# The first q panel projected one channel block at a time, the layer's embeddings projected later, and GpSimd's tensor work moved to VectorE

## The chip, the core and the metric

The kernel runs on one core of a Trainium2 chip. Its engines work at the same time, each through its own list of instructions in order: TensorE (PE; its weight loads are shown as PEld), VectorE (DVE), ScalarE (ACT), GpSimd (POOL) and SyncE (SP), whose queue starts all of this kernel's transfers. The metric is the device time of one execution, in microseconds (us).

## The reference, cut to what matters

One decoder layer on 512 tokens of 1024 channels, in float32:

```python
h  = rmsnorm(x, g_mix);  z = h @ w_in            # 1024 -> 9728 columns
rq, rk, rv, rg, aq, ak, av, gl = split(z)
y  = rmsnorm(retention(rotate(rq), rotate(rk) * dk**-0.5, rv), ret_gn)    # 4 heads, chunks of 128
ret_branch = (silu(rg) * y) @ w_ret_out
aq, ak = rotate(rmsnorm(aq, q_gain)), rotate(rmsnorm(ak, k_gain))         # 3 groups of 4 heads of 128
att_branch = merge_by_denominators(dilated_window_attention(...) for 3 groups) @ w_att_out
x  = x + (sigmoid(g_r) * ret_branch + sigmoid(g_a) * att_branch) @ w_o
x  = x + square(relu(rmsnorm(x, g_mlp) @ w_up)) @ w_down
x  = x + sigmoid(rmsnorm(x, g_ple) @ w_ple_gate) * (p @ w_ple_proj)
```

`p` holds 256 embedding channels a token. `p @ w_ple_proj` depends on nothing else in the layer and is used only in the last line.

## The kernel before, in words

**Products.** Every product is made three times (`mm3`, L258 to L260): both operands are split into a rounded high part and the rest, and high x high, high x low and low x high are added up in one bank of PSUM. A weight arrives as a unit of 512 KB (`raw`, two or four blocks of 128 channels) and is split by `split_unit`: `whi` on ScalarE (L225), `wlo` on VectorE (L226). Six `raw` buffers and four pairs of `whi` and `wlo` are turned over, so a unit's transfer waits until an earlier unit has been split.

**Panels.** A panel is 512 output columns for all 512 tokens: 4 token tiles x 8 channel blocks x 3 = 96 products in `rows_gemm`, in two halves of four channel blocks; in the second half each token tile is finished in turn and given to `consume`. Four PSUM banks (`pg`) hold the four token tiles, and a bank is free for the next panel when `consume` has read it. The order of the panels is q, k, v for each of the three attention groups, then the retention's panels.

**The first normalization** is not applied to x before the projection. The panel is computed on x times the gain, and the token's factor `r` (`token_factors`: four squares on ScalarE with a running sum, L489, then a power on GpSimd, L493) scales each bank when it is read (`zn`, L558).

**After a q or k panel**, `consume` squares each head of `zn` (L562), takes the root on GpSimd (`rstd`, L357), scales (L564) and rotates: t1 = zn x C on GpSimd (L513), two half products with S on VectorE (L516), their sum on VectorE (L518). C and S are tables made on GpSimd (`tables`, L542) from rotation constants (`rotc`) and the gains (in `mg`). The heads are then transposed on TensorE (`heads_T`, L528).

**Delayed work.** `later(lag, ...)` puts a step into a queue; `tick`, called between groups of products, takes at most one ripe step out. The heads' transposes of a panel so fall into the second half of the next one, and a group's scores, probabilities (`pe`, `pT`) and values (`po`, L643) into the panels after its v panel.

**The start.** `setup` loads the embeddings' columns, both units of `w_ple_proj`, x by channels (four loads of 512 KB), two units of the q panel and x by tokens. `embed` splits the embeddings, then alternates the split of x (`hh` L469, `hl` L470) with the split of the q panel's units, and projects the embeddings in eight bank fills of six products, which are evacuated and stored to DRAM (`pp_dram`). Only then come `token_factors`, the tables and the q panel.

The instructions stand on each engine in the order that the tile framework's scheduler chose when the kernel was built, which need not be the order in which the code is written.

Of the kernel before, what the change touches and what calls it, by code (L numbers as in the profile page):

```python
# [24 lines left out]
H = 4  # L25
# [6 lines left out]
WARM = 4  # L32
# [43 lines left out]
class Block:  # L76


    def __init__(self, ctx, tc, a):
# [17 lines left out]
        self.pinned = False  # L97
        self.plan, self.raws, self.loaded, self.used = [], [], [], 0
# [118 lines left out]
    def split_unit(self, raw, g0):  # L217
# [5 lines left out]
        if g0 is None:  # L223
            for i in range(k) if self.pinned else [slice(0, k)]:
                self.pin(nc.scalar.activation(R(hi[:, i]), raw[:, i], AF.Copy))  # L225
                nc.vector.tensor_tensor(R(lo[:, i]), raw[:, i], hi[:, i], op=ALU.subtract)  # L226
# [35 lines left out]
    def rows_gemm(self, act, nk, consume, perm=False, group=2, need=None, wave=None, halves=False):  # L262
# [3 lines left out]
        if wave is not None:  # L266
            us = []

            def part(t, u):
                if u == 0:  # L270
                    banks[t] = self.gbank()
                wh, wl = us[u]
                for k in range(2):
                    kk = 2 * u + k
                    sh, sl = self.stat(act, kk, t, perm)
                    self.mm3(banks[t], sh, sl, wh[:, k], wl[:, k], kk == 0, kk == nk - 1)
                if u == nu - 1:
                    consume(t, banks[t])

            for m in range(NT):  # L280
                self.pinned = True
                if m >= 2:
                    wave(m)
                us += self.units(1)
                if m < NT - 1:
                    for t in range(m):
                        part(t, m)
                self.force(("h", m, 1))
                if m < NT - 1:
                    for u in range(m + 1):  # L290
                        part(m, u)
                self.pinned = False
            for t in range(NT - 1):
                part(t, NT - 1)
                part(NT - 1, t)
                self.ahead(t + 1)
            part(NT - 1, NT - 1)
            return
# [105 lines left out]
    def setup(self):  # L404
        nc, a = self.nc, self.a
        self.p_raw = self.wraw.tile([P, 1024], F32, tag="raw", name="p_raw").rearrange("p (k t) -> p k t", k=2)
        for k in range(2):
            nc.sync.dma_start(self.p_raw[:, k], a["p_cols"][k * P : (k + 1) * P])
        self.fetch(2)
# [3 lines left out]
        self.x_cols = []  # L413
# [42 lines left out]
    def embed(self):  # L456
        nc = self.nc
        pT = self.big("pT")
        hi, lo = pT[:, 0:2], pT[:, 2:4]
        self.pinned = True  # L460
        for k in range(2):
            self.pin(nc.scalar.activation(R(hi[:, k]), self.p_raw[:, k], AF.Copy))
            nc.vector.tensor_tensor(R(lo[:, k]), self.p_raw[:, k], hi[:, k], op=ALU.subtract)
        self.ahead(2)
        self.hT = self.new_act(2, "h")
        for k in range(KD):
# [4 lines left out]
            if k % 2:  # L471
                self.ahead(2 + (k + 1) // 2)
        self.pinned = False
        self.pp_dram = self.dram.tile([S, D], F32, name="pp_dram", tag="pp_dram")
# [32 lines left out]
    def rotate(self, zn, C, Sn):  # L507
# [5 lines left out]
        nc.gpsimd.tensor_tensor(v4(t1), v4(zn), bc(C, HD), op=ALU.mult)  # L513
# [24 lines left out]
    def tables(self, g, n):  # L538
        C = self.tabp.tile([P, NT, HD], F32, tag="tab", name=self.nm("C"))
        Sn = self.tabp.tile([P, NT, HD], F32, tag="tab", name=self.nm("S"))  # L540
        for o, part, gi in ((C, 0, 2 * n), (Sn, 1, 2 * n + 1)):
            ins = self.nc.gpsimd.tensor_tensor(  # L542
                o, self.rc[:, 0, :, part * HD : (part + 1) * HD],
                self.gains[:, gi, g * HD : (g + 1) * HD].unsqueeze(1).to_broadcast([P, NT, HD]), op=ALU.mult)
            if g == 0:
                self.tc.keep_in_program_order(ins)
        return C, Sn

    def att_proj(self, g, n, **kw):
        nc = self.nc  # L550
        tabs = [] if kw else [self.tables(g, n)]
# [19 lines left out]
        self.rows_gemm(self.hT, KD, consume, **kw)  # L571
# [32 lines left out]
    def attention(self, g, **kw):  # L604
        nc = self.nc
        qT = self.att_proj(g, 0, **kw)
# [58 lines left out]
    def merge(self, groups, oh, ol):  # L665
# [32 lines left out]
        def weigh(h, g):  # L698
# [11 lines left out]
            nc.gpsimd.tensor_tensor(n, accs[h], t, op=ALU.add)  # L710
# [24 lines left out]
    def retention(self):  # L735
# [10 lines left out]
        def decayed(t, k):  # L746
            if t < NT - 1:
                nc.gpsimd.tensor_tensor(v4(kd[:, t]), v4(k), kdec.unsqueeze(2).to_broadcast([P, H, HD]), op=ALU.mult)

        qT = self.ret_proj()  # L750
        for h in range(H):
            def cross(h=h):
                v = lambda t: t[:, h, P:].rearrange("p (n i) -> p n i", i=P)
                nc.gpsimd.tensor_tensor(v(qd), v(qT), qdec[:, h].unsqueeze(1).to_broadcast([P, NT - 1, P]), op=ALU.mult)
# [261 lines left out]
    def make_plan(self):  # L1016
        a, w = self.a, self.w_in
        for half in range(2):
            self.plan_rows(a["w_ple_proj"][0], 512 * half, 2)
        for g in range(NG):  # L1020
            for c in (AQ, AK, AV):
                self.plan_rows(w, c + 512 * g, KD)
        for c in (RQ, RK, RV, RG, RV + 512, RG + 512):
# [12 lines left out]
    def run(self):  # L1036
# [36 lines left out]
```

## Time and profile before

| | us |
|---|---|
| median of 3 runs (lowest, highest) | 1042.34 (1041.96, 1045.39) |
| the profiled execution, its own time | 1040.62 |
| its span, first to last instruction | 1038.9 |
| mean granted TensorE clock | 0.993 |
| TensorE busy | 1009.2 |
| VectorE busy | 664.1 |
| ScalarE busy | 460.5 |
| GpSimd busy | 142.0 |
| GpSimd: L513, L542, L710, L754, L748 (59 tensor operations) | 92.1 |

The page gives busy time by engine, the chain of work that ended last, and the costliest groups of instructions. A row of the timeline reads: start, duration, engine, line, operation, output<-inputs, shape, count, and in brackets how long the engine had been idle and what ended that. In a row of a stretch stand the busy time of TensorE, its weight loads, VectorE, ScalarE and GpSimd, each with the number of instructions, then the granted TensorE clock, the share of time that the transfer engines were busy, and GB/s. A row of waits gives the total, how often, and the longest.

### The profile page before, as it was taken

How to read it: one execution, taken by the hardware profiler on the slowest of the kernel's cores; microseconds unless marked ns; L12 is line 12 of the kernel's file. 1: busy time of each engine (PE TensorE's matmuls, PEld its weight loads, DVE VectorE, ACT ScalarE, POOL GpSimd, SP SyncE). 2: the span in 40 equal slices, each digit the busy share in tenths (PEclk: the TensorE clock that was granted, in tenths of full speed). 3: DMA queues.
4: the chain of work that ended last, by engine and by line, in shares of the span. 5: the costliest groups of instructions: out<-in, count | busy, mean ns of one | idle time of the engine just before them, and what ended most of it. 6: DMA issues, size and time to landing. Idle time of an engine off the chain costs nothing.

```text
span 1038.9 us, 12633 instructions
## 1 busy us (share of the span) xinstructions
PE 1009.2 (97%) x4772; PEld 847.0 (82%) x4772; DVE 664.1 (64%) x912; ACT 460.5 (44%) x901; POOL 142.0 (14%) x123
## 2 busy tenths in 40 slices
PE   5998989999999899999999999999999999999998
PEld 3787878988988788888888888988888888888877
DVE  5388675667586634546444444679768877967983
ACT  5443634364352332434232323565356355355461
POOL 0264043223025500000000000000000000000000
PEclk9999999999999999999999999999999999999999
DMA  9842312213321222222323422354753753845711
GB/s 345 226 136 66 100 41 77 87 61 103 101 63 59 81 82 81 82 81 62 101 82 109 175 81 82 102 183 157 231 177 117 250 163 122 261 164 180 247 63 58
DMA packets 85756, 130.90 MB, mean 126 GB/s; under 512 B 7360, under 2 KB 39616, under 8 KB 85696
## 3 DMA queue, kind: packets, MB, share of 16 engines
q1 hardware_dynamic: 85696, 130.10, 38.9%
q8 instruction: 37, 0.61, 0.3%
q14 instruction: 23, 0.19, 0.1%
HBM read 125.87 MB, written 4.21 MB: 125 GB/s over the span
## 4 chain that ended last, share of the span: by engine, by line
PE 85%; DVE 7%; issue 2%; DMA 2%; POOL 2%; ACT 1%; SPq 0%; ACTq 0%; DVEq 0%; POOLq 0%
PE pg L258 25%; PE pg L260 25%; PE pg L259 25%; DVE wlo L226 2%; PE pb L260 2%; PE pb L259 2%; PE pb L258 2%; DVE ro L516 1%; PE ph L528 1%; DMA raw<-in_w_in 1%; PE pt L367 1%; POOL r L357 1%; DMA xr<-in_x_cols 1%; PE po L643 1%; PE sc L620 1%
## 5 line engine op out<-in xcount | busy, mean ns | idle before, releaser
L226 DVE TENSOR_TENSOR wlo<-raw,whi 128x1024 fp32r<-128x1024 f32 (+1 forms) x200 | 246.2, 1244 | 97.5 <-ACT whi L225 95.9
L225 ACT ACTIVATE whi<-raw 128x1024 fp32r<-128x1024 f32 (+1 forms) x200 | 203.7, 1031 | 232.9 <-PE pg L260 101.3
L258 PE MATMUL pg<-whi,hh 128*128 128x512 f32 x480 | 201.5, 420 | 0.1
L259 PE MATMUL pg<-wlo,hh 128*128 128x512 f32 x480 | 189.2, 394 | 1.1 <-DVE wlo L226 1.1
L260 PE MATMUL pg<-whi,hl 128*128 128x512 f32 x480 | 189.0, 394 | 0.0
L357 POOL TENSOR_TENSOR r<-v,mhalf 128x4 f32<-128x4 f32 (+1 forms) x48 | 38.3, 798 | 609.7 <-DVE v L356 609.5
L260 PEld LDWEIGHTS pg<-whi,hl 128*128 128x128 f32 x480 | 98.7, 206 | 17.5
L259 PEld LDWEIGHTS pg<-wlo,hh 128*128 128x128 f32 x480 | 99.2, 207 | 15.1 <-DVE wlo L226 1.6
L258 PEld LDWEIGHTS pg<-whi,hh 128*128 128x128 f32 x480 | 98.9, 206 | 14.0 <-ACT zn L558 0.5
L258 PE MATMUL pg<-h2h,whi 128*128 128x512 f32 (+1 forms) x288 | 105.4, 367 | 0.0
L259 PE MATMUL pg<-h2l,whi 128*128 128x512 f32 (+1 forms) x288 | 105.2, 365 | 0.0
L260 PE MATMUL pg<-h2h,wlo 128*128 128x512 f32 (+1 forms) x288 | 105.2, 365 | 0.0
L259 PEld LDWEIGHTS pg<-h2l,whi 128*128 128x128 f32 x288 | 54.3, 189 | 8.8
L258 PEld LDWEIGHTS pg<-h2h,whi 128*128 128x128 f32 x288 | 54.2, 189 | 8.8
L260 PEld LDWEIGHTS pg<-h2h,wlo 128*128 128x128 f32 x288 | 54.3, 189 | 8.6
L258 PE MATMUL pg<-hh,whi 128*128 128x512 f32 x128 | 52.5, 410 | 0.0
L260 PE MATMUL pg<-hh,wlo 128*128 128x512 f32 x128 | 50.0, 390 | 0.0
L259 PE MATMUL pg<-hl,whi 128*128 128x512 f32 x128 | 49.9, 390 | 0.0
L258 PE MATMUL pg<-whi,uh 128*128 128x512 f32 x128 | 49.9, 390 | 0.0
L260 PE MATMUL pg<-whi,ul 128*128 128x512 f32 x128 | 49.9, 390 | 0.0
L259 PE MATMUL pg<-wlo,uh 128*128 128x512 f32 x128 | 49.8, 389 | 0.0
L207 DVE TENSOR_TENSOR raw<-raw,raw 128x1024 f32<-128x1024 f32 x32 | 39.0, 1220 | 12.2 <-DMA raw<-in_w_down 12.2
(179 smaller groups left out, 1761.6 us busy)
## 6 DMA issues: line engine op xcount, KB each, us to landing
raw<-in_w_down SPq DMA_DIRECT2D x80, 512.0 KB, 3.4
raw<-in_w_in SPq DMA_DIRECT2D x76, 512.0 KB, 3.8
raw<-in_w_up SPq DMA_DIRECT2D x32, 512.0 KB, 5.1
x<-in_x SPq DMA_DIRECT2D x8, 512.0 KB, 8.6
raw<-in_w_ret_out SPq DMA_DIRECT2D x8, 512.0 KB, 3.4
raw<-in_w_o SPq DMA_DIRECT2D x8, 512.0 KB, 3.4
raw<-in_w_ple_gate SPq DMA_DIRECT2D x8, 512.0 KB, 4.5
xr<-in_x_cols SPq DMA_DIRECT2D x4, 512.0 KB, 8.0
```

The source lines that it names most:

```text
L207: self.nc.vector.tensor_tensor(raw, raw, g0, op=ALU.add)
L225: self.pin(nc.scalar.activation(R(hi[:, i]), raw[:, i], AF.Copy))
L226: nc.vector.tensor_tensor(R(lo[:, i]), raw[:, i], hi[:, i], op=ALU.subtract)
L258: t.matmul(ps, sh, mh, start=first, stop=False, skip_group_check=more)
L259: t.matmul(ps, sh, ml, start=False, stop=False, skip_group_check=more)
L260: t.matmul(ps, sl, mh, start=False, stop=last, skip_group_check=more)
L357: self.nc.gpsimd.tensor_tensor(r, v, self.mhalf[:, :w], op=ALU.pow)
L367: nc.tensor.transpose(ps[:, k * P : (k + 1) * P], part[:, k * P : (k + 1) * P], self.ident)
L516: nc.vector.tensor_tensor(v4(t2)[:, :, o0 : o0 + 64], v4(zn)[:, :, i0 : i0 + 64], bc(Sn[:, o0 : o0 + 64], 64), op=ALU.mult)
L528: self.nc.tensor.transpose(ps[:, t * P : (t + 1) * P], rots[t][:, h * HD : (h + 1) * HD], self.ident)
L620: nc.tensor.matmul(sc[:, h * P : (h + 1) * P], qT[:, h, rs], kT[:, h, rs], start=True, stop=True)
L643: nc.tensor.matmul(po[:, h * P : (h + 1) * P], v[:, vt, h * HD : (h + 1) * HD], pt, start=b == 0, stop=b == len(blocks) - 1)
```

## The change

Four things are changed.

1. The q panel of the first group is made by a new function, `first_panel`. The loads of x and of the panel's four units are cut into blocks of 128 channels (256 KB each) and issued in turn, x block, weight block. Through a `hook` in `split_unit` each x block is split just ahead of its weight block. The panel's products go through the first four channel blocks with all four token tiles before the second four are taken tile by tile. `token_factors` is called between these halves.
2. `embed` is called after the first group's v panel. Its loads of p and `w_ple_proj` stand in the plan behind that panel, and its pieces are split whole. The branch of `rows_gemm` for `wave`, which nothing called, is removed.
3. The tensor operations of GpSimd, except the powers and one add, go to VectorE: t1 of the rotations (32), the tables (12), the merge's adds (8), the decayed k (3) and q (4). The add that makes `gm` in `mix` stays on GpSimd.
4. Ten warm products instead of four.

```diff
@@ setup
-        self.p_raw = self.wraw.tile([P, 1024], F32, tag="raw", name="p_raw").rearrange("p (k t) -> p k t", k=2)
-        for k in range(2):
-            nc.sync.dma_start(self.p_raw[:, k], a["p_cols"][k * P : (k + 1) * P])
-        self.fetch(2)
...
         for u in range(KD // 2):
-            v = xr[u // 2][:, 2 * (u % 2) : 2 * (u % 2) + 2]
-            nc.sync.dma_start(v, a["x_cols"][256 * u : 256 * (u + 1)].rearrange("(k p) t -> p k t", p=P))
-            self.x_cols += [v[:, 0], v[:, 1]]
-        self.fetch(4)
+            src, _ = self.plan[u]
+            raw = self.wraw.tile([P, 1024], F32, tag="raw", name=self.nm("raw")).rearrange("p (k n) -> p k n", k=2)
+            for k in range(2):
+                c = slice((2 * u + k) * P, (2 * u + k + 1) * P)
+                nc.sync.dma_start(self.x_cols[2 * u + k], a["x_cols"][c])
+                nc.sync.dma_start(raw[:, k], src[k * P : (k + 1) * P])
+            self.raws.append((raw, None))
@@ split_unit
             for i in range(k) if self.pinned else [slice(0, k)]:
+                if self.hook is not None:
+                    self.hook(i)
@@ first_panel (new)
+        self.pinned = True
+        for u in range(KD // 2):
+            self.hook = lambda i: split_x(2 * u + i)
+            us += self.units(1)
+        self.hook = None
+        self.pinned = False
+        banks = [self.gbank() for _ in range(NT)]
+        for k in range(KD // 2):
+            for t in range(NT):
+                part(t, k)
+        self.token_factors()
+        for t in range(NT):
+            for k in range(KD // 2, KD):
+                part(t, k)
+            consume(t, banks[t])
+            self.ahead(1 + t // 2)
+            self.tick()
@@ embed
+        raw = self.big("praw")[:, 0:2]
+        nc.sync.dma_start(raw, self.a["p_cols"].rearrange("(k p) t -> p k t", p=P))
         hi, lo = pT[:, 0:2], pT[:, 2:4]
+        nc.scalar.activation(R(hi), raw, AF.Copy)
+        nc.vector.tensor_tensor(R(lo), raw, hi, op=ALU.subtract)
@@ rotate (and in the same way: tables, weigh, decayed, cross)
-        nc.gpsimd.tensor_tensor(v4(t1), v4(zn), bc(C, HD), op=ALU.mult)
+        nc.vector.tensor_tensor(v4(t1), v4(zn), bc(C, HD), op=ALU.mult)
@@ run
-        self.embed()
-        self.token_factors()
         self.load_tables()
-        groups = [self.attention(g) for g in range(NG)]
+        groups = []
+        for g in range(NG):
+            groups.append(self.attention(g))
+            if g == 0:
+                self.embed()
```

How the instructions stand on the engines, at three places. In the rows, `whi` and `raw` are a weight unit and its load, `hh` the split x, `j` with `ss` a square of an x tile (with x) or of a head (with zn), numbers tell buffers apart.

ScalarE between the end of the splits and the first `zn`, before:

```order
L225 ACTIVATE whi_170<-raw_168 128x512 x2
L469 ACTIVATE hh_141<-xr_94,gcol 128x512 x2
L489 ACTIVATE j_270,ss_269<-x_103 128x1024 x2
L143 ACTIVATE pp_216<-pg_209 128x512
L143 ACTIVATE pp_236<-pg_229 128x512
L489 ACTIVATE j_270,ss_269<-x_104 128x1024 x2
L143 ACTIVATE pp_256<-pg_249 128x512
L225 ACTIVATE whi_182<-raw_180 128x512 x2
```

and with the change:

```order
L433 ACTIVATE hh_146<-xr_87,gcol 128x512
L228 ACTIVATE whi_179<-raw_103 128x512
L484 ACTIVATE j_242,ss_241<-x_108 128x1024
L228 ACTIVATE whi_293<-raw_291 128x1024
L484 ACTIVATE j_242,ss_241<-x_108 128x1024
L484 ACTIVATE j_242,ss_241<-x_109 128x1024 x2
L228 ACTIVATE whi_363<-raw_361 128x1024
L552 ACTIVATE zn_269<-pg_189,r 128x512
```

The evacuations of the embedding are gone from between the squares, and between the first and the second square now stands the split of the k panel's first unit, `raw_291`.

SyncE's queue from the x tiles to the k panel's units, before:

```order
L423 DMA x_104<-in_x 128x1024 x2
L191 DMA raw_168<-in_w_in 128x2x512
L191 DMA raw_180<-in_w_in 128x2x512
L191 DMA raw_350<-in_w_in 128x2x512
L191 DMA raw_356<-in_w_in 128x2x512
L191 DMA raw_495<-in_w_in 128x2x512
L479 DMA pp_dram<-pp_196 128x512
L191 DMA raw_501<-in_w_in 128x2x512
L440 DMA rotc_283<-in_c_rot 128x4x256 x2
```

and with the change:

```order
L392 DMA x_109<-in_x 128x1024 x2
L409 DMA rotc_134<-in_c_rot 128x4x256 x2
L413 DMA mg_137<-in_c_mask 128x512
L417 DMA mg_137<-in_q_gain 128x384
L419 DMA mg_137<-in_q_gain 128x3x64 x2
L417 DMA mg_137<-in_k_gain 128x384
L419 DMA mg_137<-in_k_gain 128x3x64 x2
L192 DMA raw_291<-in_w_in 128x2x512
L192 DMA raw_361<-in_w_in 128x2x512
```

The first k units (`raw_350` and `raw_356` before) stood ahead of the tables, the mask and the gains; now (`raw_291`, `raw_361`) they stand behind all of them.

VectorE's rotation of the first token tile of the first q panel, before:

```order
L356 TENSOR_SCALAR v_382<-ss_374 128x4
L564 TENSOR_TENSOR zn_376<-zn_376,r_383 128x512
L516 TENSOR_TENSOR ro_388<-zn_376,S_295 128x4x64 x2
L518 TENSOR_TENSOR ro_389<-ro_387,ro_388 128x512
L356 TENSOR_SCALAR v_414<-ss_406 128x4
```

and with the change:

```order
L326 TENSOR_SCALAR v_275<-ss_267 128x4
L558 TENSOR_TENSOR zn_269<-zn_269,r_276 128x512
L508 TENSOR_TENSOR ro_284<-zn_269,C_280 128x512
L511 TENSOR_TENSOR ro_285<-zn_269,S_281 128x4x64 x2
L513 TENSOR_TENSOR ro_286<-ro_284,ro_285 128x512
L326 TENSOR_SCALAR v_317<-ss_309 128x4
```

One operation is added to each tile's chain on VectorE, t1 (L508), which GpSimd did beside the two half products.

More of the change, by code (lines that the diff above doesn't have):

```diff
@@ L31 @@
 NEG = -3.0e38
-WARM = 4
+WARM = 10
 GG = (2, 4)
@@ L260, in mm3, with rows_gemm @@
         t.matmul(ps, sl, mh, start=False, stop=last, skip_group_check=more)
-    def rows_gemm(self, act, nk, consume, perm=False, group=2, need=None, wave=None, halves=False):
+    def rows_gemm(self, act, nk, consume, perm=False, group=2, need=None, halves=False):
         banks = [None] * NT
         nu = nk // 2
[L266 to L272, printed above, removed]
-                for k in range(2):
[L274 to L298, printed above, removed]
         for u0 in range(0, nu, group):
@@ L453, in load_tables, with first_panel, split_x @@
         self.gains = gv
-    def embed(self):
+    def first_panel(self, consume):
         nc = self.nc
[L458 to L464, printed above, removed]
         self.hT = self.new_act(2, "h")
-        for k in range(KD):
+        us = []
+        def split_x(k):
             g = self.gcol[:, k : k + 1]
@@ L470, in embed, with part @@
             nc.vector.scalar_tensor_tensor(R(l), self.x_cols[k], g, h, op0=ALU.mult, op1=ALU.subtract)
-            if k % 2:
-                self.ahead(2 + (k + 1) // 2)
-        self.pinned = False
+        self.pinned = True
+        for u in range(KD // 2):
+            self.hook = lambda i: split_x(2 * u + i)
+            us += self.units(1)
+        self.hook = None
+        self.pinned = False
+        banks = [self.gbank() for _ in range(NT)]
+        def part(t, k):
+            wh, wl = us[k // 2]
+            sh, sl = self.stat(self.hT, k, t, False)
+            self.mm3(banks[t], sh, sl, wh[:, k % 2], wl[:, k % 2], k == 0, k == KD - 1)
+        for k in range(KD // 2):
[8 more added lines that the diff above has]
+            self.tick()
+    def embed(self):
+        nc = self.nc
+        pT = self.big("pT")
+        raw = self.big("praw")[:, 0:2]
+        nc.sync.dma_start(raw, self.a["p_cols"].rearrange("(k p) t -> p k t", p=P))
+        hi, lo = pT[:, 0:2], pT[:, 2:4]
+        nc.scalar.activation(R(hi), raw, AF.Copy)
+        nc.vector.tensor_tensor(R(lo), raw, hi, op=ALU.subtract)
         self.pp_dram = self.dram.tile([S, D], F32, name="pp_dram", tag="pp_dram")
@@ L541, in tables, with att_proj @@
         for o, part, gi in ((C, 0, 2 * n), (Sn, 1, 2 * n + 1)):
-            ins = self.nc.gpsimd.tensor_tensor(
+            self.nc.vector.tensor_tensor(
                 o, self.rc[:, 0, :, part * HD : (part + 1) * HD],
                 self.gains[:, gi, g * HD : (g + 1) * HD].unsqueeze(1).to_broadcast([P, NT, HD]), op=ALU.mult)
-            if g == 0:
-                self.tc.keep_in_program_order(ins)
         return C, Sn
-    def att_proj(self, g, n, **kw):
+    def att_proj(self, g, n):
         nc = self.nc
-        tabs = [] if kw else [self.tables(g, n)]
+        lazy = g == 0 and n == 0
+        tabs = [] if lazy else [self.tables(g, n)]
         rots = []
@@ L602, in transpose4, with attention @@
         return pT
-    def attention(self, g, **kw):
+    def attention(self, g):
         nc = self.nc
-        qT = self.att_proj(g, 0, **kw)
+        qT = self.att_proj(g, 0)
         kT = self.att_proj(g, 1)
@@ L709, in weigh @@
             n = self.tmp("mt")
-            nc.gpsimd.tensor_tensor(n, accs[h], t, op=ALU.add)
+            nc.vector.tensor_tensor(n, accs[h], t, op=ALU.add)
             accs[h] = n
@@ L1017, in make_plan @@
         a, w = self.a, self.w_in
-        for half in range(2):
-            self.plan_rows(a["w_ple_proj"][0], 512 * half, 2)
         for g in range(NG):
@@ L1022, in make_plan @@
                 self.plan_rows(w, c + 512 * g, KD)
+            if g == 0:
+                for half in range(2):
+                    self.plan_rows(a["w_ple_proj"][0], 512 * half, 2)
         for c in (RQ, RK, RV, RG, RV + 512, RG + 512):
```

13 lines of the change are left out of this document (8 added, 5 removed).

## The prediction

> **What bounds the kernel now.** I read the page's busy line and chain first, then TensorE's own waits, then the timeline of the first 110 us.
>
> ```profile
> span 1038.9 us, 12633 instructions
> PE 1009.2 (97%) x4772; PEld 847.0 (82%) x4772; DVE 664.1 (64%) x912; ACT 460.5 (44%) x901; POOL 142.0 (14%) x123
> PE 85%; DVE 7%; issue 2%; DMA 2%; POOL 2%; ACT 1%; SPq 0%; ACTq 0%; DVEq 0%; POOLq 0%
> PE pg L258 <- ACT pp L143: 4.5, 1, 4.5
> PE po L643 <- DVE pT L147: 4.4, 1, 4.4
> PE pg L258 <- ACT whi L225: 4.3, 1, 4.3
> PE ph L528 <- DVE mt L705: 3.8, 2, 3.3
> PE pg L258 <- DVE pp L147: 3.7, 1, 3.7
> ```
>
> TensorE is the bound, 85% of the chain. No product is removed, so only its idle time and its slow-clock time can be won: three waits in the embedding projection (12.5 us), one on the first attention group's probabilities (4.4), one at the merge (3.8).
>
> ```profile
> 32.72 0.39 PE L258 MATMUL pg<-whi,hh 128*128 128x512 f32 x1
> 54.48 0.39 PE L258 MATMUL pg<-whi,hh 128*128 128x512 f32 x1
> 105.47 0.40 PE L258 MATMUL pg<-whi,hh 128*128 128x512 f32 x1
> ```
>
> These rows are the first products of the first q panel, of the first k panel, and of the second group's q panel. A panel's 96 products take 21.76 us, 0.227 each. The embedding's 48 would take 10.9, yet q starts at 32.72: some 21 us of TensorE are lost before it. I measure the change by when the second group's q panel would start, now 105.47.
>
> **The change part by part.** *First panel by channel blocks.* Per block of 128 channels ScalarE does one hh and one whi, VectorE one hl and one wlo:
>
> ```profile
> 16.31 1.32 ACT L469 ACTIVATE hh<-xr,gcol 128x512 fp32r<-128x512 f32 x2
> 17.54 1.13 ACT L225 ACTIVATE whi<-raw 128x512 fp32r<-128x512 f32 x2
> 17.13 1.41 DVE L470 SCALAR_TENSOR_TENSOR hl<-xr,gcol,hh 128x512 fp32r<-128x512 f32 x2
> 18.46 1.28 DVE L226 TENSOR_TENSOR wlo<-raw,whi 128x512 fp32r<-128x512 f32 x2
> 0.00:10.00 10.00, 4.25 (x10) 2.28 (x11) 4.12 (x7) 4.95 (x8) 0.74 (x7) 1.00 0.79 266
> 10.00:20.00 10.00, 5.90 (x20) 4.36 (x18) 5.83 (x10) 5.98 (x11) 0.00 (x0) 0.99 1.04 400
> 20.00:24.00 4.00, 2.93 (x6) 1.82 (x6) 1.24 (x3) 1.21 (x3) 0.00 (x0) 0.59 1.04 388
> ```
>
> Halved: 1.23 us of ScalarE and 1.35 of VectorE a block; 0.52 MB at 388 GB/s (last column) is 1.35 too. TensorE needs 12 x 0.227 = 2.7 a block in the first half, so it is fed. First block complete near 7 us, panel end 7 + 21.8 = 28.8, where it was 54.48. Taken alone, and with the embedding's 10.9 added back later, that would be 14.8 us won. A slow clock at the start could cost some us here, but the next wait covers it. The six added warm products lie ahead of any data: nothing.
>
> *What is late next: the token factors r.* They move behind the first half of the panel, and no bank of q can be evacuated without them (zn, scaled by r). The order rows above show ScalarE's program: one square, then whi of the k panel's first unit, then three squares. That unit's load stands on SP's queue behind the x tiles, the rotation tables, the mask and six gain loads. So r waits for a weight unit, and the unit for the gains. Bytes ahead of the gains: 4.2 (panel and x) + 2.1 + 1.05 + 0.26 = 7.65 MB; 2.66 + 4.00 MB are moved by 20 us, the rest takes 2.5: 22.5. Then the gains, 0.79 MB in 256- and 1536-byte pieces. The nearest rows are the same loads in the kernel before:
>
> ```profile
> 37.50:43.50 6.00, 6.00 (x28) 4.99 (x27) 0.00 (x0) 1.06 (x1) 0.00 (x0) 1.00 0.79 68
> 44.50:50.50 6.00, 6.00 (x28) 4.98 (x27) 3.11 (x4) 3.56 (x15) 3.72 (x3) 1.00 0.39 102
> 46.03 1.00 SPq L191 DMA_DIRECT2D raw<-in_w_in  x2
> 50.50:56.00 5.50, 5.50 (x26) 4.57 (x25) 4.22 (x8) 3.43 (x10) 2.89 (x3) 1.00 0.96 355
> raw<-in_w_in SPq DMA_DIRECT2D x76, 512.0 KB, 3.8
> ```
>
> Weight units issued at 46.03 were not moved before about 50.5: while the gains ran the queue gave 102 GB/s, afterwards 355. At 388 GB/s the gains would cost 2.0 us (lower end), at 102 they cost 7.7 (taken: same loads, same queue), at 68, a stretch that also holds the r store, 11.6 (upper end). The unit itself moves in 1.35, and I add 1.2 for its end (a lone unit lands 3.8 after issue, 2.4 of it not moving; half, an estimate). It lands at 22.5 + 7.7 + 1.35 + 1.2 = 32.8 (27.1 to 36.7).
>
> ```profile
> 28.62 1.06 ACT L489 ACTIVATE j<-x 128x1024 f32<-128x1024 f32 x1
> 29.80 1.06 ACT L489 ACTIVATE j<-x 128x1024 f32<-128x1024 f32 x1
> 31.31 1.03 POOL L493 TENSOR_TENSOR r<-v,mhalf 128x4 f32<-128x4 f32 x1 [30.01 <-DVE v L492]
> ```
>
> From there whi 1.0, three squares at 1.18 (28.62 to 29.80), v and the power 1.6: 6.2 us. Call the time of r **A**: 39.0 (33.3 to 42.9). TensorE, done at 28.8, stands idle to A + 0.7 and starts the k panel at a low clock; both lie under what follows.
>
> *VectorE's rotations.* They now start at A, not during the panel, and the heads' transposes in the k panel wait for the fourth.
>
> ```profile
> 60.30 0.16 DVE L356 TENSOR_SCALAR v<-ss 128x4 f32<-128x4 f32 x1
> 61.58 0.69 DVE L564 TENSOR_TENSOR zn<-zn,r 128x512 f32<-128x512 f32 x1 [1.12 <-POOL r L357]
> 62.31 1.86 DVE L516 TENSOR_TENSOR ro<-zn,S 128x256 f32<-128x256 f32 x2
> 64.27 0.69 DVE L518 TENSOR_TENSOR ro<-ro,ro 128x512 f32<-128x512 f32 x1
> 64.88 0.16 DVE L356 TENSOR_SCALAR v<-ss 128x4 f32<-128x4 f32 x1
> 298.97 1.28 POOL L513 TENSOR_TENSOR ro<-rz,rotc 128x512 f32<-128x512 f32 x1 [2.04 <-issue]
> 300.38 0.75 DVE L516 TENSOR_TENSOR ro<-rz,rotc 128x256 f32<-128x256 f32 x2
> ```
>
> A tile took 64.88 - 60.30 = 4.58. GpSimd's t1 goes to VectorE (0.61, as L518's spacing), but the L516 pair takes 0.75 where GpSimd has just ended (300.25) and 1.86 beside it: 4.58 + 0.61 - 1.11 = 4.08 a tile. So GpSimd's work costs VectorE nothing in these chains. From A: zn and its squares 2.1, four tiles 16.3, two wlo 2.3, a table 0.6: fourth rotation at A + 21.3. Then four heads (0.44) each with six products (1.37): k panel ends A + 28.5. VectorE's next four tiles end near A + 44.5, where TensorE's v panel (16.3 in) needs them: no wait. v ends at A + 28.5 + 23.5 = A + 52.0.
>
> *Embedding behind v.* Its raw load queues on SP behind two weight loads that wait for buffers which the second wlo of w_ple_proj frees, near A + 47; with their 2.7 us of moving and its own it lands near A + 51.5, and split by A + 53.7: 2 us of wait (0 to 4). Then 10.9 for the products; scores and evacuations run beside it. Second group's q: A + 64.9 = 103.9, where it was 105.47: **-1.6**.
>
> *Later stalls.*
>
> ```profile
> 152.08 1.29 PE L643 MATMUL po<-pT,v 128*128 128x128 f32 x8 [4.38 <-DVE pT L147]
> 155.00:160.00 5.00, 5.00 (x21) 4.09 (x20) 0.00 (x0) 1.04 (x1) 0.00 (x0) 0.86 0.00 0
> 343.27 0.66 PE L528 MATMUL ph<-ident,ro 128*128 128x128 f32 x4 [3.33 <-DVE mt L705]
> 345.00:350.00 5.00, 5.00 (x20) 4.04 (x20) 2.67 (x4) 2.36 (x4) 4.92 (x4) 0.75 0.67 191
> L710 POOL TENSOR_TENSOR mt<-mt,mt 128x512 f32<-128x512 f32 x8 | 13.3, 1658 | 14.1 <-DVE mt L705 13.9
> ```
>
> At 152 the pT copy stood behind the last of four rotations. The group's steps now begin in the embedding, so it stands behind the first: TensorE waits about 1.4 instead of 4.4, and keeps its clock (the row at 0.86 lost 0.7 in 5 us; I take twice that from 152 on): **-4.4**. At the merge the eight adds (1.66 each on GpSimd) become 0.61 on VectorE without the trips between, while VectorE takes 11 us more work there and loses some 6 of contention: I take half of 3.8 and of the slow clock's 1.25 (5 us at 0.75): **-2.5** (0 to -5). The rest of what moves from GpSimd (tables, kd, qd) lies beside TensorE at 100% busy: nothing, with its cover gone 0.6 each.
>
> Sum: -1.6 - 4.4 - 2.5 = -8.5. The profiled execution of before took 1040.6 (span 1038.9 and 1.7 around it): 1032. The median of the runs shown is 1042.34, 1.7 above it: **1033.7, say 1034**.
>
> **The rivals.** *Gains nearly free* (2.0 us): A 33.3, 5.7 more won, and the merge stall may go too: 1026. For it: other traffic could fill their gaps; against: the 102 GB/s row, where units were waiting. *Small loads run slower:* the panel's 256 KB pieces move at the 266 of the first row instead of 400 until 4.2 MB are in: 15.8 us instead of 13.9, all of it in A: 1036. The Trainium skill, "DMA: Bandwidth & Descriptors", Rules for kernel authors, asks for at least 1 MiB a DMA, which speaks for this rival; no row here has 256 KB pieces in a long stream. *VectorE becomes the bound:* the L516 pair stays at 1.86 for a reason of its own; then eight tiles cost 1.1 more each (8.9 over q and k): about 1043, no change. Against: the row at 300.38. *Slower: the gains hold r for longer.* By landing, the first two gain loads (0.29 MB) needed the time from 35.5 to 44.1:
>
> ```profile
> 35.48 0.45 SPq L448 DMA_DIRECT2D mg<-in_q_gain  x1
> 44.11 1.80 POOL L542 TENSOR_TENSOR C<-rotc,mg 128x512 f32<-128x512 f32 x1 [11.77 <-DMA mg<-in_q_gain]
> ```
>
> 8.6 us; 0.79 MB at that pace is 23, A = 54.3, TensorE idle for 26 us: -8.5 + 15.3, 1049. It decides from 16.2 us of gains on, where A passes 47.5 and nothing is left. Against: the mask and the r store were in that stretch.
>
> **How the numbers follow.** Forecast 0.55; gains free 0.14; small loads 0.11; VectorE bound 0.10; slower by the gains 0.08; the start's win lost by something unseen 0.02. Range: from the first rival, 1026, to the upper end of A (+3.9) with no gain at the merge (+2.5), 1041 rounded up; that leaves the slow rival and the worse half of the VectorE one outside. 0.3% is 3.1 us, about what this kernel's measurement can tell. Faster: forecast, gains free, small loads, and little of VectorE's: 0.80; same 0.11; slower 0.09.
>
> **What would show it.** q's last product near 29 us, then one idle of about 10 us on TensorE ended by zn; whi of the k panel started by a DMA near 33; L516 pairs at 0.75; k's heads near A + 21; the wait at po near 1.4. Wrong if TensorE's idle at the start is under 5 us or over 17, or if L516 stays at 1.86.

## The result, and the profile after

The changed kernel takes 1029.67 us (median of 4 runs, 1028.4 to 1032.18) where the kernel before takes 1042.55 (4 runs, 1041.96 to 1045.39): 0.9874 of its time, 95% interval 0.9847 to 0.9901, 12.9 us less. The forecast was 1034 and the range 1026 to 1041, so the time fell inside, 4.3 us below the point. The profiled execution took 1032.18, the slowest of its four, and the profiled execution of before (1040.62) was the fastest of its own: between the two profiles lie only 8.44 us. The working of the prediction, which was made on a profile, came to 8.5.

The page of the changed kernel, its span, busy times and first line of the chain, and then TensorE's own waits:

```profile
span 1030.4 us, 12593 instructions
PE 1010.3 (98%) x4778; PEld 847.3 (82%) x4778; DVE 654.1 (63%) x968; ACT 461.4 (45%) x898; POOL 50.3 (5%) x64
PE 83%; DVE 9%; DMA 3%; issue 2%; ACT 1%; POOL 1%; SPq 0%; ACTq 0%; DVEq 0%; POOLq 0%
PE pg L261 <- ACT zn L552: 8.5, 1, 8.5
PE pg L261 <- ACT pT L467: 2.8, 1, 2.8
PE ph L523 <- DVE ro L513: 1.1, 2, 0.6
PE po L640 <- DVE pT L148: 1.1, 1, 1.1
```

The three waits at the start, in the embedding's products, and the 3.8 at the merge are gone, and the 4.4 at `po` is 1.1. A wait of 8.5 for zn, which the prediction had announced as 10, and one of 2.8 for the split embeddings have come. VectorE took over 59 operations, has 56 instructions more and is busy 10 us *less* (664.1 before).

The start, on TensorE, ScalarE, VectorE and GpSimd in the order of time:

```profile
6.49 1.22 PE L261 MATMUL pg<-whi,hh 128*128 128x512 f32 x2 [0.58 <-ACT whi L228]
29.95 0.39 PE L263 MATMUL pg<-whi,hl 128*128 128x512 f32 x1
32.27 1.06 ACT L228 ACTIVATE whi<-raw 128x1024 fp32r<-128x1024 f32 x1 [14.16 <-DMA raw<-in_w_in]
35.10 0.68 DVE L537 TENSOR_TENSOR S<-rotc,mg 128x512 f32<-128x512 f32 x1
36.76 0.17 DVE L487 TENSOR_SCALAR v<-ss 128x4 f32<-128x4 f32 x1 [0.97 <-ACT j L484]
37.08 1.03 POOL L488 TENSOR_TENSOR r<-v,mhalf 128x4 f32<-128x4 f32 x1 [35.77 <-DVE v L487]
38.88 0.80 PE L261 MATMUL pg<-whi,hh 128*128 128x512 f32 x1 [8.54 <-ACT zn L552]
40.17 0.17 DVE L326 TENSOR_SCALAR v<-ss 128x4 f32<-128x4 f32 x1 [1.24 <-ACT j L556]
42.81 0.75 DVE L511 TENSOR_TENSOR ro<-zn,S 128x256 f32<-128x256 f32 x2
44.20 0.16 DVE L326 TENSOR_SCALAR v<-ss 128x4 f32<-128x4 f32 x1
```

The first product comes at 6.49, the q panel is done at 30.2, ScalarE waits 14.2 us for the k panel's unit to 32.3, and r is there at 38.1 (37.08 + 1.03). A rotation takes 4.03 us (40.17 to 44.20), the L511 pair in it 0.75. All this is close to what was predicted. Two marks say where the time went: the same product of the program, in both kernels at full clock, in the middle of the second group's k panel and in the middle of the twelfth panel, at the merge. Rows of before, of the changed kernel, and of an experiment below (the kernel before with nothing changed but GpSimd's work on VectorE):

```profile
160.12 0.39 PE L258 MATMUL pg<-whi,hh 128*128 128x512 f32 x1
354.39 0.48 PE L258 MATMUL pg<-whi,hh 128*128 128x512 f32 x1
```

```profile
156.64 0.39 PE L261 MATMUL pg<-whi,hh 128*128 128x512 f32 x1
345.93 0.49 PE L261 MATMUL pg<-whi,hh 128*128 128x512 f32 x1
```

```profile
153.26 0.39 PE L258 MATMUL pg<-whi,hh 128*128 128x512 f32 x1
342.51 0.48 PE L258 MATMUL pg<-whi,hh 128*128 128x512 f32 x1
```

Up to the first mark, the start and the wait at `po` together, the change won 3.5 us; it won 5.0 more at the merge and nothing behind. The old start with the work on VectorE is 3.4 us *ahead* of the changed kernel at both marks. A second profile of the changed kernel (the first experiment) has the marks at 155.11 and 344.40: there the start and the wait won 5.0, the merge 5.0 again, and the old start is 1.9 ahead. What is won at the merge is the same in both, what is won before it differs by 1.5.

### The profile page after: what moved, and what is told of

The parts are those of the page before. It is cut to its first block, busy times and chain, and to the rows that moved or that the text cites. A ratio compares the mean times of both kernels' runs of the same rounds, so it can differ in the third digit from the quotient of the medians.

```text
span 1030.4 us, 12593 instructions
## 1 busy us (share of the span) xinstructions
PE 1010.3 (98%) x4778; PEld 847.3 (82%) x4778; DVE 654.1 (63%) x968; ACT 461.4 (45%) x898; POOL 50.3 (5%) x64
## 4 chain that ended last, share of the span: by engine, by line
PE 83%; DVE 9%; DMA 3%; issue 2%; ACT 1%; POOL 1%; SPq 0%; ACTq 0%; DVEq 0%; POOLq 0%
PE pg L261 24%; PE pg L263 24%; PE pg L262 24%; DVE wlo L229 2%; DMA raw<-in_w_in 2%; PE pb L261 2%; PE pb L263 2%; PE pb L262 2%; PE po L640 1%; POOL r L327 1%; PE pt L337 1%; DMA rotc<-in_c_rot 1%; PE ph L523 1%; DVE ro L511 1%; PE sc L617 1%
## 5 line engine op out<-in xcount | busy, mean ns | idle before, releaser
L229 DVE TENSOR_TENSOR wlo<-raw,whi 128x1024 fp32r<-128x1024 f32 (+1 forms) x198 | 239.9, 1221 | 82.0 <-ACT whi L228 80.8
```

## The experiments

Each kernel was compared with the kernel before on the same chip; a time is a median, a ratio is to the kernel before.

| edit | us | ratio (95%) |
|---|---|---|
| the changed kernel again | 1029.69 | 0.9883 (0.9860 to 0.9906) |
| on it: k units loaded first | 1027.84 | 0.9864 (0.9849 to 0.9879) |
| on it: squares first | 1028.12 | 0.9864 (0.9849 to 0.9878) |
| on it: k units first and v ahead of the tables | 1020.13 | 0.9782 (0.9767 to 0.9796) |
| on it: gains without small pieces | 1025.76 | 0.9834 (0.9816 to 0.9852) |
| on it: embeddings loaded early | 1025.81 | 0.9844 (0.9829 to 0.9858) |
| on it: products in the wait before the embedding | 1029.09 | 0.9871 (0.9852 to 0.9891) |
| on it: merge's adds back on GpSimd | 1033.00 | 0.9904 (0.9888 to 0.9920) |
| on it: all 59 operations back on GpSimd | 1043.43 | 0.9999 (0.9989 to 1.0009) |
| before, all 59 operations on VectorE | 1028.86 | 0.9862 (0.9846 to 0.9879) |
| before, t1 alone on VectorE | 1038.15 | 0.9950 (0.9936 to 0.9964) |
| four edits on the changed kernel | 1019.46 | 0.9769 (0.9745 to 0.9793) |

**The changed kernel again.** No edit.

> The changed kernel itself, profiled a second time. The profiled execution of it took 1032.18 us and the three others 1028.4 to 1030.5, with a mean granted TensorE clock of 0.992 against 0.993 to 0.995. Theory (the work is the same in every execution and only the clock after a TensorE wait differs): k panel starts within 0.5 us of 38.88, embedding's first product within 0.5 us of 92.67, merge wait about 1; a faster execution shows shorter slow-clock stretches behind these waits, worth up to 3 us. Rival (transfers differ between executions): the k panel's start moves by over 1.5 us, with r. Time about 1029.7.

The k panel starts at 38.42 and the embedding at 91.91 (38.88 and 92.67 in the first profile). The first half of the q panel is 1.4 us shorter and the embedding 0.8, both by the clock. The k panel's unit is there 0.5 earlier (31.8 for 32.3) and r with it; TensorE is done with the q panel 1.4 earlier, so its wait for zn grows by 0.9. So two executions of one kernel differ mostly by where the clock is low, a little by the transfers, and one profile is good to 1 or 2 us.

### What holds r

**The k panel's units first.** The two loads go ahead of the rotation tables, the mask and the gains.

```diff
         self.setup()
+        self.fetch(6)
         self.load_tables()
```

> The first two units of the k panel are loaded ahead of the rotation tables, the mask and the gains; nothing else moves on ScalarE. Theory (r waits for a weight unit, and the unit for the gains): the unit lands near 23 instead of 32.3, r is ready near 28 instead of 38.1, the q panel's zn keeps up and the k panel starts near 30.2 with no wait and at full clock. Tables come about 2.7 us later than now, so the fourth rotation ends near 50 and the first heads of the k panel, due at 46.5, wait about 3 us. Sum -6 to -8: 1022 to 1024 us. Rival (the lead is taken back by a later wait, at the heads, the embedding or the probabilities): k panel starts near 30.2, but the group-2 panels are no more than 2 us earlier: 1028 to 1030. Rival (r is late because the x tiles land late): k panel still starts after 36: no change, 1029.7.

The unit landed at 22.3, ten us earlier, and the squares were done at 26.8. But v, the next step to r, ran at 34.1, and r was there at 36.3 (the power behind v took 1.86 us here, 1.03 in the changed kernel; why is open). On VectorE:

```profile
33.47 0.69 DVE L537 TENSOR_TENSOR S<-rotc,mg 128x512 f32<-128x512 f32 x1 [1.33 <-DMA mg<-in_k_gain]
34.08 0.16 DVE L487 TENSOR_SCALAR v<-ss 128x4 f32<-128x4 f32 x1
```

In front of v stand the k panel's tables, and those wait for the last gain. The k panel started at 37.0 and the time fell by 1.9, not by 6 to 8. None of the theories had this: the tables are among the operations that the change brought to VectorE, and there they hold r a second time.

**The squares first.** ScalarE keeps all four squares ahead of the unit's split.

```diff
-            nc.scalar.activation(j, self.x_tiles[t], AF.Square, accum_out=ss[:, t : t + 1])
+            self.tc.keep_in_program_order(nc.scalar.activation(j, self.x_tiles[t], AF.Square, accum_out=ss[:, t : t + 1]))
```

(and the split of the k panel's units kept in order behind them)

> ScalarE's four squares are kept ahead of the split of the k panel's first unit; the loads stay as they are. Theory: r is ready near 24.5, the four rotations start with the tables near 27 and are done before the heads are due; the k panel now waits for its own unit, which lands at 32.3, so it starts near 33.5 instead of 38.9, after an idle of 3.3 us. Sum -5 to -6: 1024 to 1025 us. Rival (taken back later): k panel near 33.5, time no more than 2 us lower. Rival (x tiles late): r after 34, no change.

The same rows again: the squares ended at 21.8, v ran at 31.2, and r was there at 32.6.

```profile
30.62 0.69 DVE L543 TENSOR_TENSOR S<-rotc,mg 128x512 f32<-128x512 f32 x1 [2.27 <-DMA mg<-in_k_gain]
31.23 0.16 DVE L493 TENSOR_SCALAR v<-ss 128x4 f32<-128x4 f32 x1
35.61 0.79 PE L265 MATMUL pg<-whi,hh 128*128 128x512 f32 x1 [6.70 <-ACT whi L229]
```

The k panel then waited for its own unit, whose split had come behind the first zn. 1.6 us won, not 5.

**Both holds off.** The first of these edits, and v kept ahead of the tables.

```diff
         self.setup()
+        self.fetch(6)
         self.load_tables()
@@ token_factors, and tables for the first group
-        nc.vector.tensor_scalar(v, ss, 1.0 / D, EPS, op0=ALU.mult, op1=ALU.add)
+        self.tc.keep_in_program_order(nc.vector.tensor_scalar(v, ss, 1.0 / D, EPS, op0=ALU.mult, op1=ALU.add))
-            self.nc.vector.tensor_tensor(
+            ins = self.nc.vector.tensor_tensor(
...
+            if g == 0:
+                self.tc.keep_in_program_order(ins)
```

The last part puts back an order: the kernel before kept the first group's tables in the order of the program, and the change dropped that line, which its list of four parts does not name.

> The k panel's first two units are loaded ahead of the tables and gains, as before, and besides r's variance v is kept ahead of the rotation tables on VectorE. Theory (r is held twice side by side: on ScalarE by a unit that stands behind the gains, on VectorE by the tables that wait for the gains; taking one away left the other, r ready at 36.3): r ready near 28, the zn keep up with the banks, the k panel starts at 30.2 with no wait over 0.5 us and at full clock. The q tables come at 29 to 30, so the fourth rotation ends near 49 and the first heads, due at 46.5, wait 2 to 3 us. Second half of the k panel near 41, embedding's first product 4 to 6 us before 92.67: 1022 to 1025 us. Rival (a third hold): the k panel starts after 33. Rival (the lead is given back): k panel at 30.2, but the embedding's first product no more than 2 us earlier than 92.67.

r is ready at 27.9 and the k panel starts behind the q panel without a wait. 9.5 us won against the changed kernel, more than the range expected, where one of the holds alone had given 1.9: they lie side by side, each behind the gains, and only the later one counts. The wait before the embedding (2.8 in the changed kernel) is gone as well. One wait came that was not foreseen, a third thing behind the gains, the k panel's second half of units:

```profile
35.90 1.06 ACT L228 ACTIVATE whi<-raw 128x1024 fp32r<-128x1024 f32 x1 [4.06 <-DMA raw<-in_w_in]
38.92 0.79 PE L261 MATMUL pg<-whi,hh 128*128 128x512 f32 x1 [4.50 <-ACT zn L555]
```

**The gains without small pieces.** The four loads in pieces of 256 bytes are dropped; S is made from the other gain tile, its halves swapped on VectorE.

```diff
-            for half in range(2):
-                nc.sync.dma_start(gv[:, 2 * n + 1]... [:, :, half * 64 : half * 64 + 64], ...)
@@ tables: S in two halves
+        for o, part, pieces in ((C, 0, ((0, 0, HD),)), (Sn, 1, ((0, 64, 64), (64, 0, 64)))):
```

> The four gain loads in pieces of 256 bytes are gone (0.39 of 0.79 MB, 1536 of 1792 pieces); the S tables read the other gain tile with its halves swapped instead, one more operation of VectorE for each of six tables (12 halves for 6 wholes). Orders on ScalarE and VectorE stay. Theory (both holds wait for the gains, and the gains cost by their pieces): the k panel's unit lands 4 to 6 us earlier, near 27, r near 33 instead of 38.1, TensorE's idle 3 to 4.5 instead of 8.5, k panel near 33.5: -4 to -5, 1024.5 to 1026 us. If the gains cost by bytes alone: unit 3 us earlier, -2.5 to -3. Rival (the wait is for the rotation tables or the mask, not for the gains): unit no more than 1 us earlier, time within 1 us of 1029.7.

The stretch of the transfers in which the gains fall, of the changed kernel and of this one, and the unit's split here:

```profile
25.00:28.00 3.00, 3.00 (x15) 2.49 (x14) 1.39 (x2) 0.00 (x0) 0.00 (x0) 1.00 0.53 116
```

```profile
25.00:28.00 3.00, 3.00 (x15) 2.49 (x14) 1.21 (x4) 1.58 (x2) 0.00 (x0) 1.00 1.06 385
26.42 1.06 ACT L228 ACTIVATE whi<-raw 128x1024 fp32r<-128x1024 f32 x1 [8.98 <-DMA raw<-in_w_in]
```

385 GB/s where it was 116; the unit is there 5.9 us earlier (26.4 for 32.3), the k panel starts 5.8 earlier, at 33.0, and the kernel is 3.9 faster. Half the bytes went, and 5.9 us, where the prediction had put the whole cost of the gains at 7.7: the four loads in small pieces are what costs. Whether it is the number of the pieces or their size, no run tells apart.

### The embedding

**Its load earlier**, behind the first q panel instead of the first v panel.

```diff
         qT = self.att_proj(g, 0)
+        if g == 0:
+            self.p_raw = self.big("praw")[:, 0:2]
+            nc.sync.dma_start(self.p_raw, self.a["p_cols"].rearrange("(k p) t -> p k t", p=P))
         kT = self.att_proj(g, 1)
```

> The load of the embeddings is issued right behind the first q panel instead of behind the first v panel. Theory (the load's place on SyncE's queue makes the 2.8 us wait before the embedding, and that wait makes the slow clock of 0.72 and 0.60 in the 10 us behind it, some 3.4 us): wait under 0.5, full clock, -5 to -6: 1024 to 1025 us. Rival (the next limit, split of the embeddings or its weights, is right behind): the wait falls to no less than 1.5 and the slow clock stays, -1 at most. The load moves 0.5 MB ahead of the k panel's units, which may cost 1.4 us there.

The wait is gone, the clock is 1.00 from 85 to 105 us, and 3.9 us are won. Wait and clock go together here, so a second kernel was to part them.

**Products in the wait.** Eleven products into a spare bank.

```diff
@@ embed
+        spare = self.bank("spare")
+        for _ in range(11):
+            nc.tensor.matmul(spare, self.stat(self.hT, 7, 3, False)[0], self.loaded[self.used - 1][0][:, 1], start=True, stop=True)
```

> Eleven products more, into a bank that nothing reads, stand on TensorE between the first v panel and the embedding, where it waits 2.8 us for the split of the embeddings; the output is unchanged. Theory (behind an idle of 2.5 us and more the products come at 0.43 instead of 0.227 us for some 3.4 us, and that is a second price beside the wait): the first products of the embedding come at 0.227, second group's q starts 2.5 to 3.5 us earlier than 113.1 (111.6 in the second profile): 1026.5 to 1027.5 us. Rival (the slow clock has another cause, such as the mix of operand shapes or the load of the chip): products at 0.43 all the same, 1029.7.

Two stretches from the start of the embedding, of the changed kernel and of this one (the first number after the five busy times is the clock):

```profile
90.00:95.00 5.00, 2.29 (x5) 1.38 (x6) 2.35 (x3) 3.43 (x4) 0.00 (x0) 0.72 0.03 9
95.00:100.00 5.00, 5.00 (x19) 4.19 (x18) 2.71 (x5) 0.60 (x1) 0.00 (x0) 0.60 0.71 202
```

```profile
90.00:95.00 5.00, 4.16 (x17) 2.84 (x16) 3.19 (x4) 4.04 (x5) 0.00 (x0) 1.00 0.02 5
95.00:100.00 5.00, 5.00 (x28) 4.33 (x28) 4.25 (x7) 1.76 (x9) 0.00 (x0) 1.00 0.88 243
```

Fed, TensorE keeps its clock in this profile. The second group's q starts at 109.9, where it was 113.1 and, in the second profile, 111.6; from the embedding's first product it is 18.1 us, where it was 20.5 and 19.7. But a wait of nearly that length can pass without the low clock, too. In the experiment with the gains, where nothing was fed:

```profile
86.49 0.50 PE L261 MATMUL pg<-whi,pT 128*128 128x512 f32 x1 [2.44 <-ACT pT L463]
85.00:90.00 5.00, 2.98 (x12) 2.16 (x13) 3.53 (x4) 4.04 (x5) 0.00 (x0) 1.00 0.04 8
90.00:95.00 5.00, 5.00 (x28) 4.37 (x27) 4.22 (x8) 2.10 (x9) 0.00 (x0) 1.00 0.90 257
```

There, too, it is 18.1 us to the second group's q (86.49 to 104.59). With the merge's adds on GpSimd the wait is 2.1 and the clock behind it 0.84 and 0.81; with the k units first the wait is 2.1 as well, and the clock 1.00. So the low clock is a price that a wait of 2 to 3 us has in some executions and not in others, and one profile with the products does not show that they kept the clock up. In the time they do not show either: 1029.09, an interval that covers the changed kernel's. What the low clock costs on the mean of many executions stays open.

### What GpSimd's work costs

**The merge's adds back.**

```diff
-            nc.vector.tensor_tensor(n, accs[h], t, op=ALU.add)
+            nc.gpsimd.tensor_tensor(n, accs[h], t, op=ALU.add)
```

> The merge's eight adds go back to GpSimd, all else as changed. Theory (the whole gain of 5.0 us seen between the eleventh and the twelfth panel comes from the adds' trips to GpSimd): a wait of 3 to 4 us at the merge's transposes and the slow clock behind it return: 1034 to 1035 us. Rival (it comes as well from the rotations beside the merge, which GpSimd no longer does): half of it, 1032.

3.3 us lost, between the two theories. Its waits at the merge:

```profile
PE ph L523 <- DVE hT L148: 1.5, 1, 1.5
PE ph L523 <- DVE mt L702: 1.0, 1, 1.0
```

1.0 for the merge and 1.5 for a copy of heads, where the kernel before has 3.8. Between the two marks this kernel loses 3.1 us against the changed one (154.83 and 347.19), so the adds carry some two thirds of the 5.0 won there. The rest goes by something else that GpSimd no longer does; the rotations beside the merge are the likely part, which is not shown.

**All 59 operations on VectorE in the kernel before**: part 3 of the change and nothing else.

> The kernel before with one part of the change alone: the 59 tensor operations of GpSimd on VectorE. Theory: the merge stall goes (-5.0), the rotations of a tile take 4.1 instead of 4.6, the wait at the first values stays at 4 us or falls by the 1 to 2 us that four rotations gain; the start stays: -5 to -7, 1035.5 to 1037.5 us. Rival (VectorE becomes the bound, half products stay at 1.86 a pair): no gain outside the merge, or slower than 1040.

13.8 us won: as much as the whole change, and twice what was expected. Between the two profiles lie 11.7 of it, 6.9 up to the first mark and 5.0 from there to the second; the other 2 are there because the profiled execution of before took 2 us less than the median that the 13.8 are counted from. Its busy line, and its wait at the first values:

```profile
PE 1005.5 (98%) x4772; PEld 845.2 (82%) x4772; DVE 653.9 (64%) x971; ACT 461.4 (45%) x901; POOL 50.2 (5%) x64
147.49 1.16 PE L643 MATMUL po<-pT,v 128*128 128x128 f32 x8 [1.11 <-DVE pT L147]
```

The wait at `po` is 1.1, as in the changed kernel, though the embedding stands at the start and the group's steps come when they always came. Gone too are the merge's wait and two that stand in the kernel before ahead of the second group:

```profile
92.35 0.50 PE L259 MATMUL pg<-wlo,hh 128*128 128x512 f32 x1 [1.14 <-DVE wlo L226]
98.41 0.33 PE L528 MATMUL ph<-ident,ro 128*128 128x128 f32 x1 [1.59 <-DVE ro L518]
```

These end on VectorE and on its rotations; the prediction's sum has no term for them.

**The change without that part**: the start, the embedding's place and the warm products alone.

> The change without its part on GpSimd: the 59 tensor operations are on GpSimd again; the first panel, the place of the embedding and the warm products are as changed. The other half alone gave 1028.9 us, the whole change 1029.7, before 1042.6. As the prediction has it (the wait at the first values goes because the group's steps begin in the embedding, the rotations lose 0.5 us a tile, the merge stall is back): wait at the first values 1.1 to 1.4, merge stall 3 to 4, k panel near 39: 1035 to 1037 us. Rival (the wait at the first values went because GpSimd's share of the rotations went): it is 4 us or more: 1039 to 1041. Rival (the two halves only add up): 1043.4.

1043.43 against 1043.90: nothing won, to a tenth of a per cent. The third theory, that the halves only add up, gave 1043.4. Its rows:

```profile
41.36 1.85 DVE L511 TENSOR_TENSOR ro<-zn,S 128x256 f32<-128x256 f32 x2
60.90 0.48 PE L523 MATMUL ph<-ident,ro 128*128 128x128 f32 x1 [3.29 <-DVE ro L513]
144.35 1.16 PE L640 MATMUL po<-pT,v 128*128 128x128 f32 x8 [1.94 <-DVE pT L148]
```

The wait at `po` does fall, to 1.9, as the prediction's mechanism says. But with the pair at 1.85 the rotations are late for the k panel's heads by 3.3, and the merge stall is back.

**t1 alone on VectorE**, on the kernel before.

```diff
-        nc.gpsimd.tensor_tensor(v4(t1), v4(zn), bc(C, HD), op=ALU.mult)
+        nc.vector.tensor_tensor(v4(t1), v4(zn), bc(C, HD), op=ALU.mult)
```

> The kernel before with one operation moved: t1 of the 32 rotations goes from GpSimd to VectorE. All 59 moved operations gave 13.8 us on the kernel before (1028.9 against 1042.7), and the merge's eight adds 3.3 of the 13.0 of the whole change. Theory (GpSimd's t1 slows the half products beside it, 1.86 instead of 0.75 a pair, so the rotations' chain is shorter without it, and the waits behind the rotations go): a pair at 0.75, a tile at 4.1 instead of 4.6, the wait at the first values 1.1 instead of 4.4, the merge stall stays: -8 to -10, 1033 to 1035 us. Rival (the tables on GpSimd, which stand ahead of the roots of the next panel, hold it as well): a wait of 2 to 4 us at the first values stays, 1036 to 1040. Rival (the gain is the merge's and the order's): less than 3 us.

4.9 us, not 8 to 10: the rival with the tables came true. The merge's 3.8 stay, and the wait at the first values falls only to 2.4:

```profile
148.03 1.16 PE L643 MATMUL po<-pT,v 128*128 128x128 f32 x8 [2.42 <-DVE pT L147]
```

With 3.3 for the adds (measured on the changed kernel), some 5.6 of the 13.8 are left to tables, kd and qd, or to the parts together. The marks place a part of it: with t1 alone the first comes at 154.52, 5.6 ahead of before, where all 59 operations are 6.9 ahead; the second at 349.48, 4.9 ahead, where all 59 are 11.9 ahead. So t1 is most of what is won up to the first mark and nothing of what is won at the merge; the rest was not taken apart. The cost itself is seen in one group on VectorE, before and in the changed kernel (busy time, and mean ns of one half product; with t1 alone moved the mean is 509):

```profile
L516 DVE TENSOR_TENSOR ro<-zn,S 128x256 f32<-128x256 f32 x48 | 43.9, 954 | 0.7
```

```profile
L511 DVE TENSOR_TENSOR ro<-zn,S 128x256 f32<-128x256 f32 x48 | 18.1, 418 | 0.0
```

### A version that beats both

Both holds off, the gains small, the embeddings loaded early.

> Four edits at once on the changed kernel: the k panel's first two units ahead of the tables and gains, v ahead of the tables on VectorE, the gains without their 256-byte pieces, the embeddings' load behind the first panel. The first two gave 1020.1 us; what was left there was a wait of 4.5 us in the k panel, where zn of the third bank stood on ScalarE behind units that the gains held. Theory (that third hold goes with the gains' small pieces): no TensorE wait over 1 us before the second group, v panel ends near 81: 1014 to 1016.5 us. Rival (VectorE's rotations and splits are the next limit at the k panel's heads): a wait of 2 to 4 us at the heads takes most of it, 1018 to 1020.

1019.46, 0.9769 of the kernel before and not clearly better than both holds off (0.9782). The third hold went, and the rival's limit came in its place: VectorE's rotations are late for the k panel's heads.

```profile
50.66 0.48 PE L519 MATMUL ph<-ident,ro 128*128 128x128 f32 x1 [3.49 <-DVE ro L509]
```

## Why the prediction was right, and where it was wrong

**The first panel by blocks: right.** First product at 6.49 for 7, the panel's end at 30.2 for 28.8; nine products at the low clock make the difference, as was allowed for. The blocks moved at 396 to 402 GB/s between 10 and 20 us, so the rival of slow small loads is out: the kernel before, with loads of 512 KB, has 400 in that stretch. The rule that was quoted for the rival (the Trainium skill, "DMA: Bandwidth & Descriptors", Rules for kernel authors) asks for at least 1 MiB a load. No run here tries loads of that size at the start; between 256 and 512 KB in a stream the size made no difference.

**The token factors: the number right, the account half.** r came at 38.1 for 39.0, the unit at 32.3 for 32.8, TensorE's idle was 8.5 for 10. But the prediction put it all on ScalarE's order. The tables, one of which it costed at 0.6, stood ahead of v on VectorE as well. With ScalarE's hold off they kept r back, to 36.3 with the units first and to 32.6 with the squares first: one hold off gave less than 2 us each time, both off gave 9.5. That the gains cost by their loads in small pieces is shown. (The bytes ahead of the gains add up to 7.6 MB, not 7.65; that is 0.1 us.)

**The rotations: the size right, its worth wrong.** 4.03 us a tile for 4.08, the pair at 0.75, the fourth rotation at A + 20.8 for A + 21.3. The step that failed is the sentence drawn from it, that GpSimd's work costs VectorE nothing in these chains. That it costs nothing to take over was right; that each chain gets half a microsecond a tile shorter was used for the new start alone and never followed through the old waits, the wait at `po`, the merge and the two near 92 and 98 us, and the tables, kd and qd were put down at nothing. The 2 x 2 of experiments says what it is worth: 1043.4 and 1042.6 with the work on GpSimd, 1029.7 and 1028.9 with it on VectorE. The whole gain is part 3.

**The embedding behind v: the wait right, its follower missed.** The embedding's first product came at A + 54.6 for A + 54.0, after a wait of 2.8 for 2. The products then took more than 10.9:

```profile
92.67 0.80 PE L261 MATMUL pg<-whi,pT 128*128 128x512 f32 x1 [2.78 <-ACT pT L467]
98.36 1.38 PE L617 MATMUL sc<-hT,hT 128*128 128x128 f32 x8
99.50 0.48 PE L261 MATMUL pg<-whi,pT 128*128 128x512 f32 x1
100.98 1.89 PE L623 MATMUL sc<-hT,hT 128*128 128x256 f32 x8
102.51 0.58 PE L261 MATMUL pg<-whi,pT 128*128 128x512 f32 x1
113.14 0.48 PE L261 MATMUL pg<-whi,hh 128*128 128x512 f32 x1
```

20.5 us from the first row to the last. 1.1 and three times 1.5 of it are scores, 0.1 a transpose, which stood behind this mark before; 14.6 are left for 10.9. Four experiments with the clock at 1.00 there took 18.1 for the same stretch, so the low clock is some 2.4 of the 3.7 too many; the rest lies in small gaps behind the wait and behind the scores. So the second group's q starts, like for like, 1.8 us later (113.14 - 5.87 against 105.47) where 1.6 earlier was forecast; in the second profile of the changed kernel it is 0.2 later. The start loses as much as it wins: before, 21.8 us to the q panel beside the embedding's products and 3.0 in waits near 86 (0.24), 92 and 98 us; after, 6.5 to the first product, 1.9 and 2.7 of low clock in the q and the k panel, 8.5 for r, 0.6 at the heads, 2.8 and 3.7 at the embedding.

**The wait at the first values: the size right, the credit wrong.** From 1.8 behind to 3.5 ahead, 5.3 us, where 4.4 was forecast. Either half of the change brings the wait down by itself, to 1.9 and 1.1, and the stretch from the second group's q to the first mark with it, by 4.7 and 4.8 us, like for like. So the mechanism of the prediction works, but the start without part 3 has that q 5.4 later, and all is lost again; the work on VectorE wins it without that.

**The merge: mis-sized.** Half of the stall and of its low clock was taken, 2.5; the whole went, 5.0.

**The sum.** +1.8 - 5.3 - 5.0 is -8.5 between the two profiles, against -1.6 - 4.4 - 2.5. Errors of +3.4, -0.9 and -2.5 cancelled. By the second profile it is +0.2 - 5.2 - 5.0, or -10.0: that the errors cancel to nothing is the clock of one execution. The medians lie 12.9 apart because the profiled execution of before took 1.9 us less than its median and that of the changed kernel 2.5 more; 1.7 were added for the first, and the second could not be known. The clock goes some way with this: it was 0.993 in the profiled execution of before and 0.987 to 0.989 in most of the others that list it; in that of the changed kernel it was 0.992, the lowest of its four. So the forecast's nearness is in part luck, and so is the range: the one rival on VectorE had it become the bound, and none had it win the whole.

## What to carry to other kernels

An operation that runs beside another on a shared resource is priced by what it does to the other one: take the neighbour's time with and without it from the same trace, and follow the difference through every wait behind that chain. When a start is shortened, what stood far ahead of its need now stands at the end, and every queue on which it stands counts, not only the first that is found; a hold that is taken away alone may show nothing because a second lies beside it. Part a change into its halves before saying which of them won.

## What the runs showed of the hardware

GpSimd's operations with two inputs slowed VectorE's beside them by more than they spared it: 59 operations, 92.1 us on GpSimd, moved to VectorE, make VectorE's busy time 10 us shorter (664.1 to 653.9 with nothing else changed). A half product takes 0.42 us alone, 0.95 on the mean before, up to 1.5. The Trainium skill says in "SBUF — State Buffer", Who interferes with whom, that an operation of VectorE with two inputs in SBUF contends with one of GpSimd that reads it; the traces agree (0.75 for a pair alone, 1.85 beside t1).

Loads that repeat one row of DRAM over all partitions in pieces of 256 bytes held the transfers to 116 GB/s (up to 147 in other profiles) where the same stretch without them moved 385.

Around a TensorE wait of 2.8 us the clock was 0.72 and 0.60 in two stretches of 5 us in one execution, 0.92 and 0.74 around 2.5 us in another, and 0.84 and 0.81 around 2.1 us in a third. It was 1.00 around 2.4 and 2.1 us in two more, and where eleven products filled the wait. So in these runs the length of such a wait alone did not decide.
